# Steps of the next block's choice, or an empty step, put where the router weights' staging buffer is written out

## The chip, the cores and the metric

One Trainium2 chip, one of its cores. The time is device microseconds (us) of one execution, the median of the runs given. TensorE (PE) multiplies, VectorE (DVE) and ScalarE (ACT) do elementwise work, GpSimd (POOL) issues gathers of rows, SyncE (SP) issues most other transfers; each engine takes its instructions in the order in which they stand.

## What is computed

One layer of a streaming encoder for 1024 prompt tokens and 128 sample tokens: nine blocks of 128 tokens, blocks 0 to 7 of the prompt and block 8 of the samples. Cut to what matters here:

```python
xn = rmsnorm(x); q, k, v, x_r, g, gate_a, gate_r = split(xn @ w_in)
x = x + (sigmoid(gate_a) * (attention(q, k, v) @ w_ba) + sigmoid(gate_r) * (rg_lru(conv(x_r)) * gelu(g) @ w_bl)) @ w_o
# PEER, for each token t and each of 8 heads:
xt = rmsnorm(x); s1, s2 = (xt @ wq) @ keys1, (xt @ wq) @ keys2        # 128 scores each
top 16 of s1, top 16 of s2, top 16 of their sums -> expert e = i1 * 128 + i2, weight g = softmax
x = x + sum over the 8 * 16 experts of  g * gelu(u[e] . xt) * v[e]
```

## The kernel before

The mixer (everything up to the scores) runs in three passes over groups of blocks: (0, 1, 8), (2, 3, 4), (5, 6, 7). Each pass has these stages: LRU, gates, attention, then the projections `w_ba`, `w_o` and `wq` ("the projection stretch", 32 projections one behind the other). A projection (`proj`, L164 on) loads 512 KB of weights (`raw`), casts them to `hi` on ACT (L158), loads the precomputed rest `lo` (L159, 512 KB) in the second and third pass, and does 24 matmuls (L170 to L172). There are four buffers for `raw` and three for `hi` and `lo`, so the load of `lo` for a projection waits for the last matmul of the projection three before it.

After a pass, each of its blocks has to choose its experts. Blocks 1, 8, 2, 3, 4 are "dense": every expert is computed for their tokens later, and a table G_d of router weights (tokens by all 16384 experts) is built for them. This choice and building is put-off work: a list `fill` of steps, which the next pass takes from the front, one at a time, at its beats (a beat after each projection and each attention unit; how many steps are due follows from the length of the list and the work that is left).

- Choice of a block (`select`, 15 steps): eight `head` steps (top 16 of the scores), `candidates`, two `pick`, `ranks`, two `lookup`, `weights`. `weights` puts one more step, the block's table, `TAB_LATE` places from the front of the list.
- Table (`tables`, L878 on): PE turns the indices and weights (L886), ACT and DVE make `tab` of them (L889 to L899), SP writes it to HBM (`tab_d`, L900).
- Building G_d of a block (`build_g`, 17 steps): 16 parts of 8 tokens and a last step. The first part reads the table back (`tab`, L984). A part makes one-hot matrices on DVE, five operations (L998 to L1002, in two buffers each); the step after it issues its products on PE (`pg`, L1013, L1014), which ACT copies into the staging buffer `st` (L1016). There is one `st`, of 32 tokens: after every fourth part SP writes it out (`G_d<-st`, L1018, 2 MB in 8192 pieces of 256 B), and the next part's copy into it has to wait until that transfer has landed.

Before, the list of a pass is: the rest of block 0's choice (first time), the choices of all the group's blocks, then the building of all its dense blocks. The order on each engine is made at build time: a scheduler plays the program through with estimates of its own and lets an instruction pass another where it believes that one not ready. So the list sets where a step becomes available, and the scheduler where its instructions stand.

The dense stage (2040 to 3780 us in the profile) multiplies all experts for the five dense blocks; the other four blocks gather rows of `u` and `v` one expert at a time (L942, L963 on DVE; block 0's already during the second and third pass).

Of the kernel before, what the change touches and what calls it, by code (L numbers as in the profile page):

```python
# [35 lines left out]
GROUPS = ((0, 1, SB), (2, 3, 4), (5, 6, 7))  # L36
DENSE = (1, SB, 2, 3, 4)
# [7 lines left out]
PROJ_US = 3.9  # L45
PACE = ((0,) * 5, (1, 1, 1, 1, 1), (1, 1, 1, 1, 1))
CARRY = (0, 0, 0)
TAB_LATE = 9
THIRD = (0, 1, 2)
CV_TAGS = (2, 5)  # L50
GATES = 3
# [19 lines left out]
def kernel(ctx, tc, a):  # L71
# [117 lines left out]
    fill = deque()  # L189
# [11 lines left out]
    def tick(n=1):  # L201

        for _ in range(n):
            if fill:
                fill.popleft()()
# [546 lines left out]
    def make_tables(b):  # L752
        if b in pending:
            pending.pop(b)()

    def table_parts(tab):
        h = tab.bitcast(F16)
        return h[:, 0:128], h[:, 128:256], tab[:, 128:192].bitcast(BF16), h[:, 384:512], h[:, 512:640]

    def select(b, q_=""):  # L760
# [96 lines left out]
        def weights():  # L857
# [12 lines left out]
            if b in DENSE:  # L870
                pending[b] = lambda: tables(ii, gf)
                fill.insert(min(TAB_LATE, len(fill)), lambda: make_tables(b))
            else:
# [7 lines left out]
        def tables(ii, gf):  # L881


            pt = ps_p.tile([128, 4, 128], F32, name="tr", tag="pp")
            for n, src in enumerate((ii[0], ii[1], gf)):
                T.transpose(pt[:, n, :], src, ident)  # L886
            tab = tk.tile([128, 320], F32, name="tab", tag="cand")
            i1, i2, pw, hi, lo = table_parts(tab)
            S.copy(i1, pt[:, 0, :])  # L889
            S.copy(i2, pt[:, 1, :])  # L890
            wt = tk.tile([128, 128], F32, name="wt", tag="sh")
            S.copy(wt, pt[:, 2, :])
            ma = tk.tile([128, 128], F32, name="ma", tag="m1")
            bits = wt.bitcast(U32)
            V.tensor_scalar(ma.bitcast(U32), bits, 0x007fffff, 0x46000000, op0=ALU.bitwise_and, op1=ALU.bitwise_or)
            V.tensor_scalar(bits, bits, 0x7f800000, None, op0=ALU.bitwise_and)
            V.tensor_copy(pw, wt)
            S.copy(hi, ma)
            V.tensor_tensor(lo, ma, hi, op=ALU.subtract)  # L899
            nc.sync.dma_start(tab_d[b], tab)  # L900
# [73 lines left out]
    def build_g(gp, b):  # L974

        n0 = 4 * DENSE.index(b)
        st = {}

        def part(c, tb):
            def go():  # L980
                if c == 0 and tb == 0:
                    make_tables(b)
                    st["t"] = gp["st"].tile([128, 320], F32, name="tab")
                    nc.sync.dma_start(st["t"], tab_d[b])  # L984
                if tb == 0:
                    st["s"] = gp["st"].tile([128, 128, 32], F32, name="st")
                i1, i2, pw, hi, lo = table_parts(st["t"])
                sg = st["s"]
                t = c * 32 + tb * OH_T

                def row(x):
                    return x[:, t:t + OH_T].rearrange("p (g t) -> p g t", t=2).unsqueeze(2).to_broadcast(
                        [128, OH_T // 2, 128, 2])

                ow = gp["oh"].tile([128, OH_T // 2, 128, 2], BF16, name="ow")
                oh = gp["oh"].tile([128, OH_T // 2, 128, 2], F16, name="oh1")
                ol = gp["oh"].tile([128, OH_T // 2, 128, 2], F16, name="oh2")
                V.tensor_tensor(ow, gp["iota"], row(i2), op=ALU.is_equal)  # L998
                V.tensor_tensor(ow, ow, row(pw), op=ALU.mult)
                V.tensor_tensor(oh, gp["iota"], row(i1), op=ALU.is_equal)  # L1000
                V.tensor_tensor(ol, oh, row(lo), op=ALU.mult)
                V.tensor_tensor(oh, oh, row(hi), op=ALU.mult)  # L1002
                later.append(lambda: products(c, tb, ow, oh, ol, sg))
                if len(later) > 1:
                    later.popleft()()
            return go

        def products(c, tb, ow, oh, ol, sg):
            for j0 in range(0, OH_T, 4):
                pg = ps_p.tile([128, 4, 128], F32, name="pg", tag="pp")  # L1010
                for j in range(4):
                    g, e = divmod(j0 + j, 2)
                    T.matmul(pg[:, j, :], ow[:, g, :, e], oh[:, g, :, e], start=True, stop=False)  # L1013
                    T.matmul(pg[:, j, :], ow[:, g, :, e], ol[:, g, :, e], start=False, stop=True)  # L1014
                t = tb * OH_T + j0
                S.activation(sg[:, :, t:t + 4], pg.rearrange("p t i -> p i t"), ACTF.Copy, scale=2.0 ** -13)  # L1016
            if tb == 32 // OH_T - 1:
                nc.sync.dma_start(G_d[:, :, n0 + c], sg.rearrange("p (a i) t -> p a i t", i=GCH))  # L1018

        later = deque()  # L1020
        return [part(c, tb) for c in range(4) for tb in range(32 // OH_T)] + [lambda: later.popleft()()]

    def dense(dp):
# [79 lines left out]
        for c in range(nch):  # L1103
# [13 lines left out]

    mp = {nm: es_m.enter_context(tc.tile_pool(name=nm, bufs=bufs, reuse_waits="tile"))
          for nm, bufs in (("big", 2), ("s", S_BUFS), ("kv", 2), ("b", 2), ("c", 4))}
    es_g = ExitStack()  # L1120
    es_prm = ExitStack()
    gp = {}
# [36 lines left out]
    for n, blocks in enumerate(GROUPS):  # L1159
        phase[0] = n  # L1160
        if n:
            if not gp:
                gp["iota"] = iota = g_p.tile([128, OH_T // 2, 128, 2], F16, name="iota", tag="g5")
                P.iota(iota, pattern=[[0, OH_T // 2], [1, 128], [0, 2]], base=0, channel_multiplier=0,
                       allow_small_or_imprecise_dtypes=True)
                gp["st"] = es_g.enter_context(tc.tile_pool(name="st", bufs=1, side="right", reuse_waits="tile"))
                gp["oh"] = es_g.enter_context(tc.tile_pool(name="oh", bufs=2, side="right", reuse_waits="tile"))
            for b in GROUPS[n - 1]:
                if b in DENSE:
                    fill.extend(build_g(gp, b))  # L1170
        t0 = sum(len(g) for g in GROUPS[:n]) * 128
        with ExitStack() as es:
            if SB in blocks:
                mp["q"] = es.enter_context(tc.tile_pool(name="q", bufs=2, side="right", reuse_waits="tile"))
            xn = mixer(mp, n, t0, xn)
        tick(max(0, len(fill) - CARRY[n]))
        for b in SELECT[n]:
            if b in AT_ONCE:
                fill.extend(late_picks[b])
            else:  # L1180
                _, rest, heads = select(b)
                fill.extend(heads + rest)
    u0 = g_p.tile([128, KT, 128], F32, name="u0", tag="g5")
    nc.sync.dma_start(u0, a["peer_ut"][0])
    marks.clear()
# [126 lines left out]
```

## Time and profile before

| | |
|---|---|
| median of 3 runs (3871.3 to 3889.72) | 3872.69 us |
| profiled execution, its own time | 3881.13 us |
| its span | 3879.3 us |
| PE busy, share of the span | 3626.3 us, 93% |
| DVE busy | 3047.9 us, 79% |
| transfers `G_d<-st`, each to landing | 20 of 2 MB, 17.2 us |

The second pass runs from about 640 to 1300 us of the span, the third from about 1300 to 2040 us. In the second, attention ends near 1090 us, in the third near 1830 us; the projection stretch follows. Before the change the building of blocks 1 and 8 lies at 930 to 1315 us and that of 2, 3 and 4 at 1620 to 2045 us. Idle time of an engine is read with what ended it; it costs something where PE, which is busy nearly throughout, is the one that idles.

### The profile page before, as it was taken

The page shows a single profiled execution, that of the slowest core. Times are in us where ns is not written, and L with a number is a line of the kernel's source. Part 1 is how long each engine was busy: PE and PEld are TensorE (multiplying, and loading weights), DVE is VectorE, ACT ScalarE, POOL GpSimd, SP SyncE. Part 2 cuts the span into 40 slices and gives each one's busy share as a digit, 9 for nine tenths or more (in the row PEclk, how much of TensorE's full clock was granted, in tenths as well). Part 3 has the DMA queues.
Part 4 walks back from the last instruction along what each step waited for, and adds up shares of the span by engine and source line. Part 5 has one row for each costly group of instructions (what it writes and reads, how often), then busy time and mean ns, then how long its engine had stood idle before and what let it go on. Part 6 is the DMA issues. An engine that isn't in the chain of part 4 may idle for free.

```text
span 3879.3 us, 59562 instructions
## 1 busy us (share of the span) xinstructions
PE 3626.3 (93%) x21775; PEld 3257.9 (84%) x21775; DVE 3047.9 (79%) x6332; ACT 1560.1 (40%) x2699; POOL 1422.6 (37%) x1094
## 2 busy tenths in 40 slices
PE   8998899999988899988888989999999999999998
PEld 7877699877778887777778878999999999999997
DVE  8433357967876688987769999998888998888997
ACT  7554345645634564555343222322222223222222
POOL 0000100122222012322220666665675665675662
PEclk9999899999999999999999999999999999999999
DMA  7778888888999988898996999999998999998995
GB/s 258 252 241 294 282 294 282 299 324 275 292 362 355 308 299 313 302 295 287 334 347 221 341 326 340 325 350 331 354 341 313 343 346 334 333 345 324 346 341 206
DMA packets 558422, 1208.05 MB, mean 311 GB/s; under 512 B 205360, under 2 KB 281520, under 8 KB 558128
## 3 DMA queue, kind: packets, MB, share of 16 engines
q1 hardware_dynamic: 380560, 638.23, 47.5%
q0 software_dynamic: 147456, 536.94, 38.4%
q10 hardware_dynamic: 30112, 29.09, 2.2%
q8 instruction: 170, 2.79, 0.3%
q14 instruction: 124, 1.02, 0.1%
HBM read 1066.15 MB, written 137.94 MB: 310 GB/s over the span
## 4 chain that ended last, share of the span: by engine, by line
PE 66%; DVE 16%; DMA 11%; ACT 5%; issue 2%; POOL 0%; ACTq 0%; SPq 0%; DVEq 0%; POOLq 0%
PE S L1085 19%; PE pp L170 13%; PE pp L172 13%; PE pp L171 13%; DMA G_d<-st 3%; DVE row L942 3%; PE S L529 2%; PE pp L543 1%; DMA row<-peer_u,ei 1%; PE pt L458 1%; DVE x L963 1%; DVE lo L137 1%; DMA row<-peer_v,ei 1%; DMA bias<-bias_p 1%; DMA lo<-lo_w_in 1%
## 5 line engine op out<-in xcount | busy, mean ns | idle before, releaser
L915 POOL DMA_INDIRECT row<-peer_u,ei x512 | 704.4, 1376 | 1170.3 <-DVE row L942 509.4
L915 POOL DMA_INDIRECT row<-peer_v,ei x512 | 691.0, 1350 | 786.8 <-DVE x L963 528.7
L963 DVE SCALAR_TENSOR_TENSOR x<-row,q,x 128x1024 f32<-128x1024 f32 x512 | 654.8, 1279 | 25.1 <-DMA row<-peer_v,ei 18.2
L170 PE MATMUL pp<-xd,hi 128*128 128x320 f32 x2048 | 635.8, 310 | 16.0 <-ACT wf L1048 12.4
L942 DVE SCALAR_TENSOR_TENSOR row<-row,xt 128x1024 f32<-128x1024 f32 x512 | 612.5, 1217 | 38.5 <-DMA row<-peer_u,ei 37.2
L172 PE MATMUL pp<-xd,lo 128*128 128x320 f32 x2048 | 634.4, 310 | 4.5 <-DVE lo L137 4.5
L171 PE MATMUL pp<-xd,hi 128*128 128x320 f32 x2048 | 634.7, 310 | 0.0
L170 PE MATMUL pp<-xn,hi 128*128 128x384 f32 x1344 | 481.2, 359 | 12.7 <-ACT hi L158 7.2
L171 PE MATMUL pp<-xn,hi 128*128 128x384 f32 x1344 | 464.3, 345 | 0.8 <-DVE xn L137 0.8
L172 PE MATMUL pp<-xn,lo 128*128 128x384 f32 x1344 | 462.5, 345 | 1.0 <-DMA lo<-lo_w_in 1.0
L136 ACT CAST hi<-raw 128x1024 fp32r<-128x1024 f32 x223 | 234.0, 1050 | 454.6 <-PE pp L171 358.4
L137 DVE TENSOR_TENSOR lo<-raw,hi 128x1024 fp32r<-128x1024 f32 x223 | 272.2, 1221 | 174.4 <-ACT hi L136 166.7
L170 PEld LDWEIGHTS pp<-xd,hi 128*128 128x128 f32 x2048 | 386.6, 189 | 25.5 <-ACT wf L1048 15.2
L1085 PE MATMUL S<-vh,wh 128*128 128x512 f32 x1280 | 396.8, 391 | 4.8 <-DVE acc L1093 2.7
L1085 PE MATMUL S<-vl,wh 128*128 128x512 f32 x1280 | 395.6, 390 | 1.0 <-DVE vl L137 1.0
L1085 PE MATMUL S<-vh,wl 128*128 128x512 f32 x1280 | 388.0, 392 | 8.7 <-DVE wl L137 8.7
L171 PEld LDWEIGHTS pp<-xd,hi 128*128 128x128 f32 x2048 | 386.7, 189 | 6.9
L172 PEld LDWEIGHTS pp<-xd,lo 128*128 128x128 f32 x2048 | 386.7, 189 | 6.6 <-DVE lo L137 4.8
L158 ACT CAST hi<-raw 128x1024 fp32r<-128x1024 f32 x192 | 200.4, 1047 | 339.2 <-PE pp L171 236.9
L1048 ACT ACTIVATE wf<-pp 128x320 f32<-128x320 f32 x256 | 106.7, 434 | 528.9 <-PE pp L172 405.9
L170 PEld LDWEIGHTS pp<-xn,hi 128*128 128x128 f32 x1344 | 262.2, 195 | 36.7 <-issue 10.4
L1085 PEld LDWEIGHTS S<-vh,wl 128*128 128x128 f32 x1280 | 240.6, 188 | 61.1 <-DVE wl L137 11.2
(296 smaller groups left out, 6746.5 us busy)
## 6 DMA issues: line engine op xcount, KB each, us to landing
raw<-w_in SPq DMA_DIRECT2D x168, 512.0 KB, 6.1
raw<-peer_v SPq DMA_DIRECT2D x128, 512.0 KB, 6.8
raw<-peer_ut SPq DMA_DIRECT2D x127, 512.0 KB, 7.0
lo<-lo_w_in SPq DMA_DIRECT2D x112, 512.0 KB, 5.6
G_d<-st SPq DMA_DIRECT2D x20, 2048.0 KB, 17.2
gt<-G_d SPq DMA_DIRECT2D x64, 640.0 KB, 7.7
lo_w_in<-lo SPq DMA_DIRECT2D x56, 512.0 KB, 3.6
raw<-wq SPq DMA_DIRECT2D x48, 512.0 KB, 6.9
```

The lines of the kernel that those rows point to most:

```text
L136: S.copy(r32(hi), src)
L137: ins = V.tensor_tensor(r32(lo), src, hi, op=ALU.subtract)
L158: S.copy(r32(hi), raw)
L170: T.matmul(out, r32(lh), r32(rh), start=first, stop=False)
L171: T.matmul(out, r32(lh), r32(rl), start=False, stop=False)
L172: T.matmul(out, r32(ll), r32(rh), start=False, stop=last)
L529: T.matmul(s[:, m, 0:nh], st["q"][r0:r0 + 64, i * 128:(i + 1) * 128], kf[r0:r0 + 64, ko + m * nh:ko + (m + 1) * nh], start=True, stop=True)
L915: P.indirect_dma_start(out=t, out_offset=None, in_=table, in_offset=bass.IndirectOffsetOnAxis(ap=ei[:, j:j + 1], axis=0))
L942: V.scalar_tensor_tensor(u, u, 1.0, xt, op0=ALU.mult, op1=ALU.mult, accum_out=hh[:, j:j + 1])
L963: V.scalar_tensor_tensor(x2, v, q[:, j:j + 1], x2, op0=ALU.mult, op1=ALU.add)
L1048: S.activation(w[:, c1], ps, ACTF.Gelu_apprx_tanh)
L1085: T.matmul(po[:, m, :], r32(l[:, c1]), r32(r[:, m * 512:m * 512 + 512]), start=(n == 0 and q == 0 and (c == 0 or not held)), stop=(n == EC ...
```

## The change

`TAB_LATE` goes from 9 to 4. The choices of dense blocks no longer go into the list at once; they are kept in `chosen`, and the list of the next pass is put together anew. First stands the whole choice of the first dense block. Then, for each dense block: the first 6 steps of the next block's choice, and the parts of this block's building, with 3 of the other 9 steps of that choice after the parts 4, 8 and 12 (counted from 0), that is, one part after `st` became full. For the last block there is no next choice, and one empty step stands at each of these three places. The number of instructions is the same. The list has three steps more in each pass.

```diff
-TAB_LATE = 9
+TAB_LATE = 4
...
+    chosen = {}
+
+    def woven(parts, other):
+
+        out, other = other[:len(other) - 9], deque(other[len(other) - 9:])
+        for i, p in enumerate(parts):
+            out.append(p)
+            if i in (4, 8, 12):
+                out.extend([other.popleft() for _ in range(3)] if other else [lambda: None])
+        return out
+
...
-            for b in GROUPS[n - 1]:
-                if b in DENSE:
-                    fill.extend(build_g(gp, b))
+            todo = [b for b in GROUPS[n - 1] if b in DENSE]
+            fill.extend(chosen[todo[0]])
+            for b, b1 in zip(todo, todo[1:] + [None]):
+                fill.extend(woven(build_g(gp, b), chosen.get(b1, [])))
...
-                fill.extend(heads + rest)
+                if b in DENSE:
+                    chosen[b] = heads + rest
+                else:
+                    fill.extend(heads + rest)
```

What the scheduler makes of it is seen on three engines.

ACT, in the building of block 3, between the last copy into one filling of `st` and the first into the next (`p`, `pT`, `oa` are attention, `hi` the weights' cast, `mg` the output of `w_ba`). Before:

```order
L1016 ACTIVATE st_18834<-pg_19250 128x128x4
L136 CAST mg_19013<-tg_19196 128x384
L158 CAST hi_19456<-raw_19454 128x1024
L158 CAST hi_19523<-raw_19521 128x1024
L136 CAST mg_19013<-tg_19268 128x384
L136 CAST mg_19013<-tg_19338 128x384
L1016 ACTIVATE st_19231<-pg_19311 128x128x4
```

After, the first twelve rows of the same place:

```order
L1016 ACTIVATE st_18263<-pg_18828 128x128x4
L442 ACTIVATE p_18773,sum_18774<-S_18766,mx_18771 128x640
L395 ACTIVATE tg_18842<-pp_18784 128x384
L136 CAST oa_15120<-pp_18845 128x128
L459 COPY pT_18861<-pt_18862 128x512
L459 COPY pT_18861<-pt_18868 128x128
L448 ACTIVATE p_18773<-p_18773,sum_18774 128x640
L442 ACTIVATE p_18878,sum_18879<-S_18871,mx_18876 128x640
L459 COPY pT_18903<-pt_18904 128x512
L459 COPY pT_18903<-pt_18910 128x128
L442 ACTIVATE p_18920,sum_18921<-S_18913,mx_18918 128x640
L459 COPY pT_18941<-pt_18942 128x512
```

There were 5 rows between the two fillings, in the projection stretch; now there are 27, in attention. Between the other fillings that lie in attention before and after, 14 to 22 rows became 23 to 57; among those of block 8, 8, 8 and 13 became 7, 7 and 37, and among those of block 4, 9, 28 and 10 became 7, 20 and 18.

DVE, at the first part of block 8's building (`row` is a gathered row of block 0, `mg` and `tg` the output of `w_ba`, `tab` the table read back). Before:

```order
L942 SCALAR_TENSOR_TENSOR row_11185,hh_7236<-row_11185,xt_7237 128x1024
L998 TENSOR_TENSOR ow_11577<-iota_6456,tab_11574 128x1024
L1000 TENSOR_TENSOR oh1_11578<-iota_6456,tab_11574 128x1024
L999 TENSOR_TENSOR ow_11577<-ow_11577,tab_11574 128x1024
L1001 TENSOR_TENSOR oh2_11579<-oh1_11578,tab_11574 128x1024
L137 TENSOR_TENSOR oa_8099<-pp_11378,oa_8099 128x128
L1002 TENSOR_TENSOR oh1_11578<-oh1_11578,tab_11574 128x1024
```

After:

```order
L942 SCALAR_TENSOR_TENSOR row_11299,hh_7250<-row_11299,xt_7251 128x1024
L942 SCALAR_TENSOR_TENSOR row_11352,hh_7250<-row_11352,xt_7251 128x1024
L942 SCALAR_TENSOR_TENSOR row_11369,hh_7250<-row_11369,xt_7251 128x1024
L998 TENSOR_TENSOR ow_11361<-iota_6456,tab_11358 128x1024
L1000 TENSOR_TENSOR oh1_11362<-iota_6456,tab_11358 128x1024
L998 TENSOR_TENSOR ow_11501<-iota_6456,tab_11358 128x1024
L1000 TENSOR_TENSOR oh1_11502<-iota_6456,tab_11358 128x1024
L999 TENSOR_TENSOR ow_11361<-ow_11361,tab_11358 128x1024
L1001 TENSOR_TENSOR oh2_11363<-oh1_11362,tab_11358 128x1024
L999 TENSOR_TENSOR ow_11501<-ow_11501,tab_11358 128x1024
L1001 TENSOR_TENSOR oh2_11503<-oh1_11502,tab_11358 128x1024
L1002 TENSOR_TENSOR oh1_11362<-oh1_11362,tab_11358 128x1024
```

The first two parts of block 8 now stand interleaved, because both come due with the table's arrival. Right ahead of the rows after stand, of the second projection of `w_ba`, L670 (it reads the projection's result), L671 and two casts' rests (L137); on PE the products of the first part stand directly behind the matmuls of that second projection, before the third (before, some three projections stood between the attention result on which those DVE rows wait and the products). In the building of block 4 the same happens behind the first projection of `w_o`: L684, L687, one L963, then the nine rows with another L963 among them.

SP, at the table of block 4. Before, the write stood in attention, among the loads of that stage; after, it stands in the projection stretch, behind a write of `st`:

```order
L1018 DMA G_d_135<-st_18809 8192x1x64
L683 DMA xT_19684<-xT 128x384
L683 DMA xT_19727<-xT 128x384
L900 DMA tab_d4_125<-tab_19480 128x320
L159 DMA lo_19556<-lo_w_o0_5210 128x1024
L149 DMA raw_19800<-w_o 128x1024
L683 DMA xT_19795<-xT 128x384
L683 DMA xT_19865<-xT 128x384
L159 DMA lo_19624<-lo_w_o1_5249 128x1024
```

The table, its reading back and the loads of the `w_o` weights now follow a write of `st` on SP. Of the writes of `st`, five lay in the projection stretch of the second pass and six in that of the third; after the change the last of block 1's is issued while attention ends, and four and five remain there.

## Rows read from the trace of the kernel before

**Rows 1.** The page's first part: the span, and the busy time of each engine.

```profile
span 3879.3 us, 59562 instructions
PE 3626.3 (93%) x21775; PEld 3257.9 (84%) x21775; DVE 3047.9 (79%) x6332; ACT 1560.1 (40%) x2699; POOL 1422.6 (37%) x1094
```

**Rows 2.** The view of one tile, the staging buffer `st`: its instructions (duration in ns, least, median, most; first and last start), how long their engine sat idle before them and for what (us, times), who waited for them (us, times), and the time of its transfers from issue to landing.

```profile
L1016 ACT ACTIVATE st<-pg x160: 573/598/669, 963.2 to 2028.3; 128x512 f32<-128x512 f32 x160
L1018 SPq DMA_DIRECT2D G_d<-st x20: 524/525/651, 985.4 to 2028.9; - x20
...
  DMA G_d<-st: 31.7, 10
...
  PE pg L1013: 15.2, 7
...
  PE pp L170: 12.8, 9
...
  PE pt L458: 5.8, 2
...
DMA to landing us min/median/max: 14.7/17.2/20.7
```

**Rows 3.** Busy time by stretch: the stretch, its length, busy us of PE, PEld, DVE, ACT, POOL with instructions, the granted clock of TensorE (1 is full speed), the busy share of the DMA engines, GB/s.

```profile
1090.00:1300.00 210.00, 178.69 (x1157) 168.91 (x1155) 133.64 (x337) 85.71 (x145) 36.35 (x32) 0.93 1.01 348
...
1480.00:1630.00 150.00, 139.15 (x834) 111.15 (x832) 142.64 (x491) 84.56 (x179) 42.10 (x41) 0.95 0.88 300
1630.00:1830.00 200.00, 176.80 (x1293) 144.92 (x1293) 166.54 (x303) 112.14 (x234) 53.45 (x41) 0.93 0.90 281
1830.00:2040.00 210.00, 173.52 (x1184) 165.19 (x1181) 146.53 (x304) 81.51 (x134) 45.49 (x34) 0.93 1.01 344
```

**Rows 4.** The timeline of PE in the third pass's attention, the rows before which it idled for the copies into `st`: start, us, instruction, idle time before it and what ended it.

```profile
1659.40 0.81 PE L458 MATMUL pt<-ident,p 128*128 128x128 f32 x5 [1.18 <-ACT st L1016]
...
1695.24 1.33 PE L458 MATMUL pt<-ident,p 128*128 128x128 f32 x5 [4.59 <-ACT st L1016]
...
1733.39 0.44 PE L170 MATMUL pp<-xn,hi 128*128 128x384 f32 x1 [1.42 <-ACT st L1016]
...
1811.94 0.33 PE L458 MATMUL pt<-ident,p 128*128 128x128 f32 x1 [2.82 <-ACT tg L395]
```

**Rows 5.** The timeline of SP in the third pass's projection stretch: start, how long the issue held SP, instruction.

```profile
1841.51 0.53 SPq L1018 DMA_DIRECT2D G_d<-st  x1
1842.17 14.60 SPq L668 DMA_DIRECT2D mr<-mr_d  x1
1856.86 0.38 SPq L159 DMA_DIRECT2D lo<-lo_w_ba  x1
...
1878.22 0.52 SPq L1018 DMA_DIRECT2D G_d<-st  x1
1881.25 10.04 SPq L159 DMA_DIRECT2D lo<-lo_w_o  x1
```

**Rows 6.** The timeline of PE in the same stretch.

```profile
1859.43 0.69 PE L170 MATMUL pp<-oa,hi 128*128 128x384 f32 x1 [8.15 <-ACT st L1016]
...
1897.01 0.27 PE L1013 MATMUL pg<-oh,ow 128*128 128x128 f16 x1 [4.83 <-ACT st L1016]
```

**Rows 7.** The page's DMA issues: KB of each, median us from issue to landing, of a load of `lo`.

```profile
lo<-lo_w_in SPq DMA_DIRECT2D x112, 512.0 KB, 5.6
```

**Rows 8.** The view of the tile `tab_d`: landing times of the table's write and of its reading back, ten transfers together.

```profile
DMA to landing us min/median/max: 2.2/6.4/8.2
```

**Rows 9.** Busy time by stretch, as in rows 3, for two short stretches behind an idle PE.

```profile
1859.00:1866.00 7.00, 6.57 (x22) 6.57 (x23) 0.00 (x0) 1.85 (x4) 0.23 (x1) 0.55 1.02 402
1694.50:1698.00 3.50, 2.76 (x11) 2.72 (x12) 3.46 (x6) 3.41 (x8) 0.00 (x0) 0.52 0.66 256
```

**Rows 10.** Groups of DVE's instructions between 640 and 2045 us: line, engine, operation, names, shapes, count, then busy us, mean ns of one, and idle time before.

```profile
L963 DVE SCALAR_TENSOR_TENSOR x<-row,q,x 128x1024 f32<-128x1024 f32 x128 | 163.0, 1273 | 12.8 <-DMA row<-peer_v,ei 12.5
L942 DVE SCALAR_TENSOR_TENSOR row<-row,xt 128x1024 f32<-128x1024 f32 x128 | 154.6, 1217 | 8.5 <-DMA row<-peer_u,ei 8.2
...
L1000 DVE TENSOR_TENSOR oh<-iota,tab 128x1024 f16<-128x1024 f16 x80 | 54.8, 685 | 57.9 <-PE pg L1013 57.8
L998 DVE TENSOR_TENSOR ow<-iota,tab 128x1024 bf16<-128x1024 f16 x80 | 54.6, 682 | 3.5 <-DMA tab<-tab_d 3.4
...
L1002 DVE TENSOR_TENSOR oh<-oh,tab 128x1024 f16<-128x1024 f16 x80 | 54.1, 679 | 0.0
...
L687 DVE SCALAR_TENSOR_TENSOR xt<-x2c,par,xt 128x384 fp32r<-128x384 f32 x16 | 9.8, 614 | 4.1 <-ACT xt L686 4.1
L684 DVE SCALAR_TENSOR_TENSOR x2c<-pp,xT 128x384 f32<-128x384 f32 x16 | 8.9, 555 | 11.4 <-PE pp L172 11.4
L137 DVE TENSOR_TENSOR mg<-tg,mg 128x384 fp32r<-128x384 f32 x16 | 8.9, 554 | 6.4 <-ACT mg L136 6.4
...
L670 DVE SCALAR_TENSOR_TENSOR tg<-tg,pp 128x384 f32<-128x384 f32 x16 | 8.8, 550 | 18.7 <-PE pp L172 18.7
```

## The prediction

> **What bounds the kernel now.** I read the page's first part: PE is busy 93% of the span, DVE 79% [rows 1], so time is won or lost where PE idles. Then the table by stretch: in the projection stretches of the second and third pass PE idles 31.3 and 36.5 of 210 us, in the third pass's attention 23.2 of 200, in a stretch without building 10.9 of 150, or 7% [rows 3]. So the building costs something, mostly in the projection stretches, where the DMA engines are full (share 1.01). Then the view of the staging buffer `st`: one transfer out of it takes 17.2 us to land, ACT sat idle 31.7 us for it at ten places, and PE waited 15.2 + 12.8 + 5.8 = 33.8 us for the copies into `st` [rows 2]. The change puts more work between one filling and the next. ACT shows only part of it, since a late copy also holds PE's result buffers.
>
> **The wait for `st`, by place.** In the third pass's attention PE idled 1.18 + 4.59 + 1.42 + 2.82 = 10.0 us for it [rows 4]. (The last names `tg`, which stood behind a copy into `st`.) Order gives the cover there: 23 to 57 rows of ACT between fillings instead of 14 to 22; ACT is about half busy there (112 of 200 us [rows 3]), so 10 to 20 rows more are about as much as the transfer lasts past the first beat. I count all 10.0 as gone. Idling also lowers the clock: behind the gap of 4.59 us the granted clock was 0.52 for 3.5 us with PE busy 2.76 [rows 9], the 1.2 GHz level in place of 2.4, so 1.4 us lost; for four gaps I take 6. Together 16 us.
>
> In the projection stretches I count nothing for that wait. At 1881 us the issue of the next `lo` held SP for 10.04 us behind the transfer out of `st` [rows 5]; issued by 1891.3, it lands some 5.6 us later [rows 7], at 1896.9 us, an estimate. PE's idle time ended at 1897.01, by the copy into `st` [rows 6]. Two waits end together: take the one away, and the other holds PE to the same moment. At 1842 SP was held 14.60 us, the next `lo` went out at 1856.86 and landed near 1862.5, while PE idled 8.15 us to 1859.43; here some 4 us were the copies' alone [rows 5, 6]. But after the change the last transfer of block 3 stands in the same stretch with loads of `w_o` behind it, so I give this nothing either.
>
> The Trainium skill, "DMA: Bandwidth & Descriptors", section "Rules for kernel authors", says that a transfer overlaps with compute if it is issued early, work is done, and its semaphore is waited on late; by that alone all 33.8 us would go. The trace agrees for the wait and not for the time: the transfer still holds the queue. [...]
>
> **Fewer transfers in the projection stretches.** Order moves one transfer out of each: five become four and six become five. Price of one, from both sides: all idle time shared out, 31.3/5 and 36.5/6, about 6.2; less the 7% that a stretch without building idles (15 of 210), 3.2 to 3.6 [rows 3]. I take 4, nearer to the lower end, as the first contains idling that stays: 8 us for both, up to 12. The attention that takes them in has DMA share 0.90 and three times as long between projections; I add nothing.
>
> **New waits of PE for the first products of a block.** With the table four steps from the front and the building close behind, the first two parts come due at once, and their DVE rows stand interleaved, so the first part is ready only after nine operations.
>
> Block 8: behind the second `w_ba` projection DVE does L670 and L671 (0.55 each), two L137 (0.55 each), three L942 (1.22 each), nine one-hot operations (0.68 each) [rows 10]: 2.2 + 3.65 + 6.15 = 12.0 us, while PE has nothing between that projection and the products. The table's reading back follows on SP a load that waits for the same projection, and lands some 6.4 us after its issue [rows 8]; DVE gets to the first one-hot row after 5.9 us, so this adds a microsecond or two at most, which I leave to the bounds.
>
> Block 4: behind the first `w_o` projection L684, L687, two L963, nine operations: 0.56 + 0.61 + 2.55 + 6.15 = 9.9 us, and only a transpose on PE.
>
> Blocks 3 and 1, in attention, by the same count of rows and less the matmuls that stand between: 5.7 and 3.5 us.
>
> Sum 31 us. In the projection stretches two gaps of 10 us bring low clock, as behind the gap of 8.15: 6.57 us of PE at 0.55 [rows 9], 3 us each, 6. Against that, these gaps swallow waiting for weights that follows in the same stretch, in which `lo` is now on time: at most one transfer's price each, 4 + 4 = 8. I take 29 us. Bounds: 12, if the attention gaps vanish in others and the two large ones are half covered; 45, if block 4's table, whose write now stands on SP behind a transfer out of `st`, comes 14.6 us late [rows 5] and nothing is swallowed. Everything else moved (selection on DVE, tables, `ranks`) is the same instructions in another place, so I cost it at nothing; it is hidden as long as DVE, 95% busy in the densest stretch (142.64 of 150 [rows 3]), isn't asked for more there. The six empty steps issue nothing.
>
> **Sum.** 16 + 8 = 24 us won, 29 lost: +5. The profiled execution, 3881.1 us, would become 3886; it lies 8.4 over the median of 3872.7, against which I state the time: 3878.
>
> **Rivals.** *The cover works and the bursts don't bite:* all 33.8 us for `st` go, with the clock behind them (8) and up to 4 for moved transfers, and the first products meet a PE that waits for weights anyhow, so that only 15 of the 31 remain: 31 faster, 3842. (It is where the skill's rule on overlap, above, would take it.) For it: the wait is measured, the bursts are only read from an order. Against: in the projection stretch the `lo` lands when the copy is free. It decides if PE, at a block's first product, has idled for weights just before. *Slower:* the bursts at full price, 31 + 6, and block 4's table held on SP behind the transfer, 8 more, against 16 won: +29, 3902. For it: no row of PE stands between; against: the weights catch up in a gap. It decides when block 4's table write is issued more than 10 us after its data is there. *It doesn't do what it says:* the 20 transfers of 17.2 us only change places, the waits for `st` turn into waits for weights of the same length, and the bursts disappear in these: 3873.
>
> **How the numbers follow.** Forecast 0.42, the third rival 0.10, both within 0.5% (3853 to 3892; about what a measurement of this kernel tells from no change); faster 0.26; slower 0.22. The forecast's own range by its bounds: won 16 to 28, lost 12 to 45, 3857 to 3902; the whole range, reaching into the faster case, 3848 to 3903.
>
> **What would show it.** In the profile after: ACT's idle for `G_d<-st` below 10 us (right for the cover); PE gaps of about 10 us before L1013 with DVE as cause, at the second `w_ba` and the first `w_o` projection (right for the bursts); PE's idle in the projection stretches not below 55 us together (now 67.8). Wrong, if these gaps are below 4 us, or if PE's gaps behind the transfers there shrink though SP is still held 10 us and more.

## The result and the profile after

The changed kernel takes 3915.86 us, median of 5 runs (3908.71 to 3923.18), beside 3874.78 for the kernel before on the same chip: ratio 1.0101, 95% interval 1.0086 to 1.0115. It is slower by 1.0%; the forecast said 3878 and no change, and the time lies outside the range. The profiled execution has a span of 3914.1 us, 34.8 more than that of the kernel before. (That one took 3881.1 us, some 6 over its median, so profiles show a little less than the medians do.) One run of one experiment, e3_empty_only, took 10891.3 us and is left out of its ratio. The page's first part of the kernel after, beside [rows 1]:

```profile
span 3914.1 us, 59577 instructions
PE 3615.2 (92%) x21775; PEld 3256.2 (83%) x21775; DVE 3049.5 (78%) x6332; ACT 1559.9 (40%) x2699; POOL 1424.6 (36%) x1094
```

All engines do the same work, and PE is busy for 11.1 us less; what grew is the time in which PE has nothing to do, from 253.0 to 298.9 us. First the staging buffer, the view of tile `st`, as in [rows 2] (the first two rows are idle time of ACT, the others of PE for the copies into `st`):

```profile
  PE pg L1014: 59.7, 36
  DMA G_d<-st: 11.9, 4
...
  PE pg L1013: 13.8, 7
...
  PE pt L458: 3.6, 2
  PE pp L170: 1.6, 2
```

ACT's idle time for the transfer fell from 31.7 us at ten places to 11.9 at four, and PE's for the copies into `st` from 33.8 to 13.8 + 3.6 + 1.6 = 19.0. The cover works, then. (ACT now idles 59.7 us for PE's products, before 19.7; ACT is not the bottleneck.) Now busy time by stretch, the four of [rows 3]:

```profile
1090.00:1300.00 210.00, 158.67 (x995) 151.82 (x994) 127.85 (x304) 72.64 (x122) 32.75 (x30) 0.86 0.92 318
1480.00:1630.00 150.00, 131.90 (x877) 108.08 (x876) 132.62 (x357) 78.10 (x155) 31.22 (x25) 0.92 0.82 263
1630.00:1830.00 200.00, 178.52 (x1226) 144.73 (x1227) 157.31 (x365) 117.25 (x247) 45.94 (x40) 0.94 0.86 272
1830.00:2040.00 210.00, 161.43 (x1082) 152.94 (x1081) 134.88 (x255) 76.38 (x130) 46.01 (x39) 0.88 0.96 328
```

PE idles 51.3 us in the first and 48.6 in the last, where it idled 31.3 and 36.5: the loss is in the projection stretches. These begin and end elsewhere now, so they are measured again between the same instructions, the second pass's from its first projection of `w_ba`, the third's from its fifth. They last 218 and 206 us before,

```profile
1083.00:1301.00 218.00, 185.74 (x1206) 175.32 (x1205) 139.55 (x352) 87.73 (x149) 37.70 (x33) 0.94 1.01 350
...
1839.00:2045.00 206.00, 168.33 (x1154) 159.92 (x1153) 143.03 (x300) 81.49 (x133) 41.56 (x32) 0.93 1.02 340
```

and 240 and 221 after, with the same busy time of PE:

```profile
1078.00:1318.00 240.00, 185.93 (x1187) 177.68 (x1188) 137.73 (x328) 86.91 (x147) 38.93 (x35) 0.87 0.92 315
1856.00:2077.00 221.00, 168.34 (x1110) 160.37 (x1107) 138.60 (x293) 78.63 (x130) 45.56 (x38) 0.88 0.97 323
```

That is 22 + 15 = 37 us, the whole loss. What the cover won does not show in the time: from the third pass's first projection to that fifth one 538.6 us pass before and 538.6 after, and 15.0 of the latter are a wait that is new. What PE waits for, the view of its waits over the whole kernel after (us in total, times, longest):

```profile
PE pg L1013 <- DVE oh L1002: 49.2, 8, 20.7
...
PE pg L1013 <- ACT st L1016: 13.8, 7, 3.9
PE pp L172 <- DMA lo<-lo_w_o: 12.9, 2, 11.4
```

The first row does not exist before the change: PE waits 49.2 us for one-hot operations. Five of its eight places, with 47.1 us, are the first products of the five blocks, 1, 8, 2, 3 and 4 in this order, as the timeline of PE shows (the row with `lo` stands between the last two):

```profile
887.43 0.29 PE L1013 MATMUL pg<-oh,ow 128*128 128x128 f16 x1 [3.02 <-DVE oh L1002]
...
1112.10 0.29 PE L1013 MATMUL pg<-oh,ow 128*128 128x128 f16 x1 [20.69 <-DVE oh L1002]
...
1484.43 0.23 PE L1013 MATMUL pg<-oh,ow 128*128 128x128 f16 x1 [3.59 <-DVE oh L1002]
...
1703.63 0.29 PE L1013 MATMUL pg<-oh,ow 128*128 128x128 f16 x1 [9.33 <-DVE oh L1002]
...
1887.33 0.69 PE L172 MATMUL pp<-mg,lo 128*128 128x384 f32 x1 [11.37 <-DMA lo<-lo_w_o]
...
1904.87 0.26 PE L1013 MATMUL pg<-oh,ow 128*128 128x128 f16 x1 [10.50 <-DVE oh L1002]
```

The longest, block 8's, taken apart with the timeline of DVE (PE's last matmul before it began at 1091.07 us):

```profile
1096.49 0.56 DVE L670 SCALAR_TENSOR_TENSOR tg<-tg,pp 128x384 f32<-128x384 f32 x1 [9.62 <-DMA tg<-tg_d]
1097.35 0.56 DVE L671 TENSOR_TENSOR tg<-mr,tg 128x384 f32<-128x384 f32 x1 [0.30 <-DMA mr<-mr_d]
...
1102.37 1.22 DVE L942 SCALAR_TENSOR_TENSOR row<-row,xt 128x1024 f32<-128x1024 f32 x1
1103.51 0.08 DVE L942 DVE_READ_ACCUMULATOR row<-row,xt 128x1 f32 x1
1106.53 0.69 DVE L998 TENSOR_TENSOR ow<-iota,tab 128x1024 bf16<-128x1024 f16 x1 [2.94 <-DMA tab<-tab_d]
...
1111.36 1.29 DVE L1002 TENSOR_TENSOR oh<-oh,tab 128x1024 f16<-128x1024 f16 x2
```

From 1091.4 to 1096.5, 5.1 us, DVE waits for the load of `tg`; from then to 1103.6 it does the rows that the prediction counted, and one L670 and one L671 more; 2.9 us it waits for the table's reading back; then come the nine one-hot operations.

The table itself is waited for in two blocks only, 2.9 us here and 1.4 at block 4. At block 3 it was read back long before; the timelines of SP and of DVE:

```profile
1676.01 0.42 SPq L984 DMA_DIRECT2D tab<-tab_d  x1
...
1693.94 0.68 DVE L998 TENSOR_TENSOR ow<-iota,tab 128x1024 bf16<-128x1024 f16 x1
```

What the five places have in common is that PE comes to the products before DVE is done: the first product starts 0.7 us after the start of the L1002 that it needs, in all five blocks, and that operation lasts 0.7 us. Before the change 3.6 to 96 us lay between the two starts, with other work of PE in them.

SP's timeline in the projection stretches:

```profile
1065.30 0.53 SPq L1018 DMA_DIRECT2D G_d<-st  x1
1069.30 12.41 SPq L159 DMA_DIRECT2D lo<-lo_w_ba  x1
...
1864.47 0.53 SPq L1018 DMA_DIRECT2D G_d<-st  x1
1865.74 14.75 SPq L683 DMA_DIRECT2D xT<-xT  x2
1880.58 0.38 SPq L900 DMA_DIRECT2D tab_d<-tab  x1
1881.05 0.38 SPq L159 DMA_DIRECT2D lo<-lo_w_o  x1
```

At both places SP is held behind a write of `st`, as it was in [rows 5]; what now stands behind it are the loads of `tg` on which DVE waits ahead of block 8, the table of block 4 (made by 1864.9, written at 1880.58) and the `lo` on which PE waits until 1887.33.

### The profile page after: what moved, and what is told of

It is laid out like the page before. It is cut to its first block, busy times and chain, and to the rows that moved or that the text cites. A ratio compares the mean times of both kernels' runs of the same rounds, so it can differ in the third digit from the quotient of the medians.

```text
span 3914.1 us, 59577 instructions
## 1 busy us (share of the span) xinstructions
PE 3615.2 (92%) x21775; PEld 3256.2 (83%) x21775; DVE 3049.5 (78%) x6332; ACT 1559.9 (40%) x2699; POOL 1424.6 (36%) x1094
## 4 chain that ended last, share of the span: by engine, by line
PE 61%; DVE 16%; DMA 9%; ACT 3%; issue 3%; POOL 0%; SPq 0%; ACTq 0%; DVEq 0%; POOLq 0%
PE S L1085 19%; PE pp L170 12%; PE pp L172 12%; PE pp L171 12%; DVE row L942 3%; PE S L529 2%; DMA G_d<-st 1%; DVE x L963 1%; PE pp L543 1%; DMA row<-peer_v,ei 1%; PE pt L458 1%; DMA raw<-wq 1%; DVE lo L137 1%; ACT hi L158 1%; DMA row<-peer_u,ei 1%
## 5 line engine op out<-in xcount | busy, mean ns | idle before, releaser
L963 DVE SCALAR_TENSOR_TENSOR x<-row,q,x 128x1024 f32<-128x1024 f32 x512 | 655.3, 1280 | 27.1 <-DMA row<-peer_v,ei 19.1
L942 DVE SCALAR_TENSOR_TENSOR row<-row,xt 128x1024 f32<-128x1024 f32 x512 | 612.8, 1219 | 38.7 <-DMA row<-peer_u,ei 38.6
L137 DVE TENSOR_TENSOR lo<-raw,hi 128x1024 fp32r<-128x1024 f32 x223 | 272.5, 1223 | 167.8 <-ACT hi L136 152.7
L1085 PEld LDWEIGHTS S<-vl,wh 128*128 128x128 f32 x1280 | 240.2, 188 | 57.7 <-DVE vl L137 6.3
```

What stands on the lines that cost most here:

```text
L137: ins = V.tensor_tensor(r32(lo), src, hi, op=ALU.subtract)
L942: V.scalar_tensor_tensor(u, u, 1.0, xt, op0=ALU.mult, op1=ALU.mult, accum_out=hh[:, j:j + 1])
L963: V.scalar_tensor_tensor(x2, v, q[:, j:j + 1], x2, op0=ALU.mult, op1=ALU.add)
L1085: T.matmul(po[:, m, :], r32(l[:, c1]), r32(r[:, m * 512:m * 512 + 512]), start=(n == 0 and q == 0 and (c == 0 or not held)), stop=(n == EC ...
```

## The experiments

Ratios are to the kernel before, run on the same chip (its medians there lie between 3872.6 and 3876.1 us); 0.0010 is 3.9 us. All microseconds that "come back" or are lost below are differences of these ratios, and by the intervals such a difference is good to some 8 us. "One-hot" is PE's wait L1013 for L1002 in the profiled run.

| kernel | median us | ratio, interval | one-hot us |
|---|---|---|---|
| the change | 3915.86 | 1.0101 (1.0086 to 1.0115) | 49.2 |
| e1_tab0 | 3868.58 | 0.9988 (0.9978 to 0.9998) | 3.0 |
| e2_no_empty | 3890.62 | 1.0037 (1.0026 to 1.0049) | 37.0 |
| e3_empty_only | 3909.53 | 1.0088 (1.0070 to 1.0107) | 3.1 |
| e4_tab4_only | 3888.19 | 1.0031 (1.0018 to 1.0044) | 1.2 |
| e6_pool_write | 3892.41 | 1.0044 (1.0028 to 1.0060) | 41.4 |
| e7_tab0_b8 | 3901.66 | 1.0070 (1.0053 to 1.0086) | 25.5 |
| e8_tab0_b4 | 3901.23 | 1.0069 (1.0053 to 1.0084) | 41.1 |
| e9_tab0_no_empty | 3853.68 | 0.9946 (0.9928 to 0.9965) | 0.9 |
| e10_empty_end | 3871.47 | 0.9985 (0.9971 to 0.9999) | 2.1 |
| e11_pool_no_empty | 3861.65 | 0.9949 (0.9932 to 0.9966) | 1.0 |
| e12_tab0_b3 | 3897.67 | 1.0052 (1.0035 to 1.0068) | 45.4 |
| e13_empty_end9 | 3864.57 | 0.9972 (0.9960 to 0.9983) | 8.0 |
| e14_pace94 | 3863.48 | 0.9968 (0.9957 to 0.9980) | 2.5 |

The theory: what is lost is the wait for a block's first products, because its table is made too close ahead of its first part; the weaving itself gains. By the list, no step stands between the table and the first part of blocks 8 and 4, two steps for blocks 1 and 2, six for block 3. The rivals: the weaving costs, `TAB_LATE` 4 costs in any order, the empty steps cost, the transfers that hold SP cost wherever the table stands.

**e1_tab0.** The table right behind the choice: four steps ahead of the first part of blocks 8 and 4, six of blocks 1 and 2, ten of block 3.

```diff
-TAB_LATE = 4
+TAB_LATE = 0
```

> The changed kernel with TAB_LATE 0 in place of 4: the table of a block stands right behind its `weights` step, four steps ahead of its first part, so it is made and written before the first part comes due; the weaving and the empty steps stay. Theory A (the loss is the first products of blocks 8, 3 and 4 meeting PE early, because table and first two parts come due together): no gap of PE above 5 us before L1013 at the first products of blocks 8 and 4, the steps of +25 us (block 8) and +26 us (block 4) against the kernel before go, total 3865 to 3890. Theory B (the loss is that choice and building are woven into each other, so that building comes earlier in attention and the loads behind it are held): the time stays above 3905. Theory C (the gaps are the transfers out of st that hold SP's loads, wherever the table stands): at most 10 us come back, 3900 to 3910, and PE still has gaps of about 8 to 11 us that end with a load of lo.

0.0113, or 44 us, come back. In the profile the wait for one-hot operations is gone, from 49.2 us to a row near the end of the list of PE's waits:

```profile
PE pg L1013 <- DVE oh L1002: 3.0, 2, 2.2
```

As the theory has it, and neither the weaving nor the transfers by themselves. What the earlier table does is seen on the two engines: the first products of blocks 1, 8, 2, 3 and 4 now start 30.3, 11.6, 2.5, 26.7 and 0.7 us after the start of the L1002 that they need, where it was 0.7 us in all five. The first two parts stand interleaved on DVE here too, so the nine operations alone are not what costs; it costs when PE has nothing else before the products. Why six steps were too few at block 3, and four are enough at block 4, is not shown.

**e2_no_empty.** The changed kernel without empty steps.

```diff
-                out.extend([other.popleft() for _ in range(3)] if other else [lambda: None])
+                out.extend([other.popleft() for _ in range(3)] if other else [])
```

> The changed kernel without the empty steps (three fewer places in each pass's list, behind the last block's parts 4, 8 and 12). Theory A: the gaps at the first products of blocks 8 and 4 stay, 3900 to 3920. Theory D (the empty steps shift the last block's building later and with it the table and the transfers into the projection stretch's end): 3870 to 3890, and those gaps shrink below 5 us.

3890.62 is neither: 25 us come back, though the long waits stay (17.76 us at block 8, 9.47 at block 3, 8.00 at block 4, all for L1002). Of the 25 us 12.2 are these waits, which are shorter in sum. The other half has no wait to its name, and the theory did not have it.

**e3_empty_only.** The order before, with an empty step behind the parts 4, 8 and 12 of every dense block.

```diff
+    def woven(parts):
+
+        out = []
+        for i, p in enumerate(parts):
+            out.append(p)
+            if i in (4, 8, 12):
+                out.append(lambda: None)
+        return out
...
-                    fill.extend(build_g(gp, b))
+                    fill.extend(woven(build_g(gp, b)))
```

> The kernel before with TAB_LATE 9 and its list as it was, only an empty step behind the parts 4, 8 and 12 of every dense block, so that a beat without a part stands where st is written out. Theory A: cover without bursts, so the waits for st shrink (ACT idle for it from 31.7 to 10 to 20 us) and the time is 3 to 20 us below before, 3855 to 3872. Theory D (empty steps cost): 3885 or more. Theory C (the transfer's hold on SP is what costs, and cover for ACT gives nothing): 3870 to 3880, with ACT's idle time for st down and PE's unchanged.

The theory missed this by 37 us and more: it is 34 us slower than before, as the rival had it by which empty steps cost (3885 or more). The empty steps give no cover to PE: its waits for the copies into `st` are 13.6 + 11.9 + 8.8 = 34.3 us, for 33.8 before. The profiled execution took 3901.9 us and shows 21 of the 34. Where they lie is odd: the dense stage begins at 2042.9 us, before at 2044.0, and ends 21 later. In it PE waits longer for `wl`, a product of DVE; the view of PE's waits from 2044 us on, e3_empty_only, and then before:

```profile
PE S L1085 <- DVE wl L137: 21.1, 8, 5.4
```

```profile
PE S L1085 <- DVE wl L137: 8.7, 6, 3.6
```

That is 12 of the 21. Why steps that issue nothing, all of them ahead of the dense stage, do this is not settled.

**e4_tab4_only.** The order before with `TAB_LATE` 4 alone.

```diff
-TAB_LATE = 9
+TAB_LATE = 4
```

> The kernel before with TAB_LATE 4 in place of 9 and nothing else. In the old list the table of every block but the last has whole choices of other blocks behind it, so its lead stays long. Theory A: 3865 to 3885, no gap above 5 us at a first product. A theory that TAB_LATE 4 costs by itself (the table's transposes and write come later, whatever the order of the list): 3895 to 3915.

12 us slower, 3 above the end of what the theory allows and under the rival's; PE waits 1.2 us for one-hot operations in it. So the number 4 by itself is not what costs 44 us: it does in the woven order, in which few steps are left between `weights` and the first part.

**e6_pool_write.** The write of `st` on GpSimd's queue.

```diff
-                nc.sync.dma_start(G_d[:, :, n0 + c], sg.rearrange("p (a i) t -> p a i t", i=GCH))
+                nc.gpsimd.dma_start(G_d[:, :, n0 + c], sg.rearrange("p (a i) t -> p a i t", i=GCH))
```

> The changed kernel with the write of st to G_d issued by GpSimd's queue in place of SP's, all else as it was. If SP held behind that write is a large share of the loss (loads of weights and the gather of w_ba's output behind it come 10 to 15 us late): the gap of PE at the first products of block 8 falls from 20.69 to about 12 us, the one that ends with lo for w_o from 11.37 to under 4, and the time to 3890 to 3906. If the burst of DVE alone decides: both stay within 3 us, 3910 to 3922. If POOL's row gathers are held instead of SP's loads, DVE waits for rows of block 0 and the time is 3920 or more.

22 us come back, within the range, but not where it was expected. The timeline of PE:

```profile
1112.15 0.29 PE L1013 MATMUL pg<-oh,ow 128*128 128x128 f16 x1 [20.91 <-DVE oh L1002]
...
1872.24 0.69 PE L172 MATMUL pp<-mg,lo 128*128 128x384 f32 x1 [6.02 <-DMA lo<-lo_w_o]
```

The wait for `lo` at block 4 is halved; block 8's stays, and block 3's falls from 9.33 to 4.57 us. SP is free at block 8, but DVE comes to L670 hardly earlier (1095.38 us, 1096.49 in the change), since three L942 stand ahead of it that start only at 1089.02 to 1094.23 us, the first after a wait for its row; and DVE waits 4.70 us for the table, 2.94 in the change. So block 8's 20.69 us are not put down to SP alone: take it away, and other waits end at nearly the same moment.

**e7_tab0_b8, e8_tab0_b4, e12_tab0_b3.** Lead 0 for one block alone, the others as in the change: block 8 in the diff, 4 and 3 in the other two.

```diff
-                fill.insert(min(TAB_LATE, len(fill)), lambda: make_tables(b))
+                fill.insert(min(0 if b == 8 else TAB_LATE, len(fill)), lambda: make_tables(b))
```

> The changed kernel with the lead of the table changed for block 8 alone (0 places instead of 4 behind its `weights`); blocks 1 to 4 keep theirs. If the first products of block 8 cost the 25 us that the start of the projections shows: 15 to 30 us under the changed kernel, 3886 to 3901, with the gap of 11.37 and 10.50 us at block 4 still there. If gaps only move (what is won here is given back at the next wait for weights): within 8 us of it, 3908 to 3922.

> The changed kernel with the lead of the table changed for block 4 alone (0 places instead of 4); everything up to 1700 us of the span is the same order as the changed kernel. If block 4's start costs the 26 us that the start of the projections shows: 15 to 30 us under the changed kernel, 3886 to 3901, and with the result for block 8 the two add up to the 47 us that lead 0 for all gave. If gaps only move: 3908 to 3922.

> The changed kernel with the lead of the table changed for block 3 alone (0 places instead of 4). PE waits 9.33 us there for the first products, in attention. If that is lost for good: 6 to 12 us under the changed kernel, 3903 to 3910, and with 12 each for blocks 8 and 4 some 10 of the 44 us stay for blocks 1 and 2 and the clock. If attention makes it up (other work on PE comes later, the next wait is longer): within 4 us, 3911 to 3920.

12, 12 and 19 us come back, each give or take 8, below the range expected of the first two and above that of the third, though by less than that error. Together they make 43, where lead 0 for all gives 44; with errors of this size the agreement is partly luck. Each takes its own wait away; in e8_tab0_b4 the first projection of `w_o` waits half a microsecond, with block 4's products ahead of it:

```profile
1884.80 0.22 PE L1013 MATMUL pg<-oh,ow 128*128 128x128 f16 x1
...
1886.30 0.41 PE L170 MATMUL pp<-mg,hi 128*128 128x384 f32 x1 [0.53 <-DVE tg L670]
```

Waits and time do not match one to one. In e7_tab0_b8 the one-hot wait falls by 23.7 us and the time by 12; in e12_tab0_b3 it falls by 3.8, since block 8's grew to 24.03 and block 4's to 12.60, and the time by 19. Up to block 8 the change, e8_tab0_b4 and e12_tab0_b3 have the same order on SP and DVE, and block 8's wait is 20.69, 22.36 and 24.03 us in their profiled executions: one wait of one execution is good to some 3 us.

**e9_tab0_no_empty.** Both: lead 0 and no empty steps, the weaving alone.

> The changed kernel with TAB_LATE 0 and without the empty steps: the weaving alone. The empty steps cost 25 us beside late tables. If they cost by themselves (they push the last block of a pass later by three beats): 3843 to 3860, faster than the kernel before by 0.5% or more. If they cost only by where they put the late table: within 8 us of TAB_LATE 0 with them, 3861 to 3877.

The fastest, 21 us under the kernel before, within what was expected if empty steps cost by themselves. It has no long wait for one-hot operations and keeps the cover in attention; the busy time by stretch, which stands beside [rows 3]:

```profile
1630.00:1830.00 200.00, 192.11 (x1380) 161.70 (x1379) 164.41 (x376) 118.90 (x243) 46.16 (x38) 0.99 0.91 299
```

PE idles 7.9 us in place of 23.2. From the third pass's first projection to its fifth of `w_ba` it now takes 507.0 us, 31.6 less than before; the waits for the copies into `st` fell there by some 8 of these, and the rest has no single wait to its name. With e1_tab0 and e2_no_empty the table of four is full: late tables cost 44 us with empty steps and 35 without; empty steps 25 with late tables and 16 without; the weaving in this order gains 21. 35 + 16 − 21 is 30 of the 39 us of the change; the other 9 come of the two together, or are error.

**e10_empty_end, e13_empty_end9, e14_pace94.** The empty steps of e9_tab0_no_empty behind the last part, three (first diff; nine in e13_empty_end9), and none with a lower pace (second diff).

```diff
+        last = not other
...
+        if last:
+            out.extend([lambda: None] * 3)
```

```diff
-            due[0] += max(0, len(fill) - CARRY[gi]) * us * w / left[0]
+            due[0] += 0.94 * max(0, len(fill) - CARRY[gi]) * us * w / left[0]
```

> The kernel of e9_tab0_no_empty (weaving, TAB_LATE 0) with three empty steps behind the last part of a pass's last block instead of between its parts: the list has the length of the one with empty steps, so the beats take steps at the same pace, but no beat without a part stands where st is written out. If the empty steps cost 16 us by the pace (a longer list makes more parts due early, in attention): 3863 to 3875. If they cost by the place between the parts: 3846 to 3860, as without them.

> The kernel of e9_tab0_no_empty with nine empty steps behind the last part of a pass's last block, three times those of e10_empty_end. If empty steps cost by the pace (a list of more steps makes the parts due earlier): more than the 15 us that three cost, 3880 or more. If three cost by chance of the order that comes out: no trend, anywhere from 3850 to 3880.

> The kernel of e9_tab0_no_empty with 0.94 of its pace: each beat counts 0.94 as many steps as due, so parts come later (about two of 102 at half of the third pass) and the last beats take what is left; the opposite of empty steps. If the pace is the cause: at or below e9_tab0_no_empty, 3835 to 3854. If what costs is any other order than this one: 3860 to 3880. If later parts pile up before the dense stage: 3870 or more with PE waiting for st after 1900 us.

Three at the end cost 15 us, as many as between the parts, so it is not the place between the parts. But nine cost 10, and a slower pace without any costs 9 (each give or take 8): no trend with the list's length, and the pace is not the cause. Five orders with early tables lie between 0.9946 and 0.9988, 16 us apart, with no one wait that would explain it; e9_tab0_no_empty is the best of them. So the 16 us that empty steps cost beside early tables are no more than the distance between such orders, and they are not shown to be a price of empty steps; nor is all of the 21 us shown to be the weaving's gain, since the five orders gain 5 to 21. (The profiled run of e10_empty_end took 3856.9 us, 15 under its median, so its waits are not compared.)

**e11_pool_no_empty.** e9_tab0_no_empty with the write on GpSimd's queue, as in e6_pool_write.

> The kernel of e9_tab0_no_empty with the write of st issued by GpSimd's queue in place of SP's. That move gave 22 us with late tables. If it gave them by freeing SP's loads behind each transfer, wherever the table stands: 3830 to 3845. If it only eased the late tables (their write and reading back stand on SP): 3848 to 3860. If the 2.8 us that GpSimd needs to issue one, and its wait for the last copy into st, hold the gathers of rows and nothing is left to ease: 3860 or more.

0.9949 beside 0.9946: no difference by the ratios. (The quotients of the bare medians, 3861.65 by 3874.14 and 3853.68 by 3872.63, would be 0.9968 and 0.9951, 7 us slower, and the time lies 2 us inside the third case, in which the gathers are held.) The 22 us of e6_pool_write are not there with early tables and no empty steps; that late tables stood behind the writes explains it, but it is argued from this pair.

## Why the prediction was wrong, step by step

**"I count all 10.0 as gone" and the price of 4 for each transfer.** The size was near. In the third pass's attention (1620 to 1856 us) PE waited 10.7 us for these copies, `tg` among them, and waits 4.2 now. In the two projection stretches the waits for `st` fall from 25.5 us, the 8.15 and 4.83 of [rows 6] among them, to 12.7, by 12.8 where 8 was taken for the moved transfers. ACT's 11.9 us miss the mark of 10 narrowly.

**"So I give this nothing either."** Right in its kind: the 8.15 us of [rows 6] are gone, and 11.37 us for `lo` stand in their place, behind the same kind of hold, 14.75 us of SP. The Trainium skill, "DMA: Bandwidth & Descriptors", section "Rules for kernel authors", has a transfer overlap with compute by early issue and a late wait. The traces agree for the buffer's own wait and not for what stands behind the transfer on SP.

**"2.2 + 3.65 + 6.15 = 12.0 us" for block 8: this failed.** The rows and their durations are nearly right, 12.7 us of the 20.69. Missing are 5.1 us until the load of `tg` has landed and 2.9 us for the table. The prediction let DVE begin when PE was done and gave the table "a microsecond or two at most". Block 3 was 9.33 for 5.7; block 4, 10.50 for 9.9, and block 1, 3.02 for 3.5, are right. Sum 43.5 for 31, and block 2, of which the prediction says nothing, adds 3.6.

**"These gaps swallow waiting for weights … 4 + 4 = 8": the step that failed most.** The largest waits of PE in the second pass's stretch before and after:

```profile
PE pp L170 <- ACT hi L158: 16.7, 10, 4.3
PE pg L1013 <- ACT st L1016: 9.3, 4, 4.6
```

```profile
PE pg L1013 <- DVE oh L1002: 20.7, 1, 20.7
PE pp L170 <- ACT hi L158: 12.0, 3, 7.9
PE tr L186 <- ACT x L699: 8.2, 1, 8.2
PE pg L1013 <- ACT st L1016: 3.7, 1, 3.7
```

And in the third pass's, before and after:

```profile
PE pg L1013 <- ACT pq L719: 14.9, 6, 6.7
PE pp L170 <- ACT st L1016: 10.6, 3, 8.1
```

```profile
PE pp L170 <- ACT pq L719: 13.7, 2, 7.8
PE pp L172 <- DMA lo<-lo_w_o: 11.4, 1, 11.4
PE pg L1013 <- DVE oh L1002: 10.5, 1, 10.5
PE pg L1013 <- ACT st L1016: 7.5, 3, 3.9
```

The wait for the weights' cast (`hi`) did shrink in the second pass, by 4.7 us. But all waits other than those for one-hot operations and for `st`, summed over all rows of these views, grew by 4.6 us there (22.6 to 27.2) and by 13.1 in the third pass (21.7 to 34.8). That is 18 us more where 8 less were taken, and 11.4 of them are the `lo` behind the held SP, the hold to which the prediction gave nothing.

The granted clock fell from 0.94 and 0.93 to 0.87 and 0.88 there; PE's busy time is the same for 1.6% and 3.8% fewer instructions, at most some 3 and 6 us as an estimate from these counts (6 were taken; it is less if the short products are what moved out).

So for the two stretches the prediction's terms give 12.0 + 9.9 + 6 − 8 − 8 = 12 us; they lost 37. Of the 25 us between, 26 are the waits that were to be swallowed and 9 the first products; against them go a cover better by 5 and the 6 for the clock, since PE's busy time did not grow. The 25 are most of the 34 by which the sum was off (+5 against 39 by the ratio). The upper bound of 45 left out the 6 us for the clock that the sum has: 31 + 6 + 14.6, less 16, would have been 3908, still below 3915.86. PE's idle time in the two windows of [rows 3], 99.9 us where the prediction asked for no less than 55, shows the same.

**The rivals.** The slower one, 3902, was the case that came: the bursts at full price, and its condition held, since block 4's table was issued 15.7 us after it was made. Its price of 8 for that table did not come at the table (DVE waited 1.4 us for it) but at the `lo` behind it on SP, 11.37. The measured time lies 14 us beyond it. It got too small a chance, as each wait was set against a gap that was to take it in, without a row that showed the two at the same moment.

**What the change does** is thus two things: weaving, which gains 5 to 21 us by the order that comes with it, and tables that come late in the list, which cost 35 to 44. The second is shown by e1_tab0 and by the pair e2_no_empty and e9_tab0_no_empty, and lies well over the 16 us between orders. What stays open is the 16 to 25 us with the empty steps, the loss of e3_empty_only in the dense stage, and by what rule the scheduler sets the products right behind DVE's operations when the table comes late.

## What to carry to other kernels

When work is put off and interleaved, look at what a later step needs from an earlier one, and at where the bounding engine's first use of it will stand: here the trip of the table through memory was the smaller part (4.3 us), and the larger was that PE came to the first products with nothing else to do while DVE was still at work on them. No one number of steps was enough everywhere (six were too few at block 3, four did at block 4), so look at the distance between the two instructions in the order itself. Do not set a new wait against an old gap unless rows show both at the same moment. And before a reordering is judged, make two or three others that should be neutral: here such orders lay 16 us apart, or 0.4% of the time, so a gain or loss below that says little about its reason.

## What the runs showed of the hardware

- The same 2 MB write holds an issuing queue by very different amounts. On SP's it took 0.5 us to issue and held the next issue for 12.41 and 14.75 us. On GpSimd's each took 2.8 us, the view of tile `st` of e6_pool_write (duration in ns: least, median, most), and in block 8's stretch no issue on SP around it took over 1.31 us. That was worth 22 us with late tables and nothing measurable with early ones and no empty steps.

```profile
L1018 POOL DMA_DIRECT2D G_d<-st x20: 2776/2785/2818, 917.6 to 2037.4; - x20
```

- Steps that issue nothing moved the time by 10 to 34 us. They change nothing but the order that the scheduler makes, and in e3_empty_only the loss showed only in the dense stage, behind all of them.
